# Block 3 of an output projection in a spare PSUM bank, and the last squares and the root of a norm moved behind the queries

## The chip, the cores and the metric

The kernel runs on one core of a Trainium2 chip. Five engines work side by side, each in the order of its own program: TensorE (PE, matrix products, with PEld for its weight loads), VectorE (DVE), ScalarE (ACT), GpSimd (POOL) and SyncE (SP, which issues transfers). They wait for each other through semaphores. The metric is the device time of one execution in microseconds, the median of the runs. PE sums products in PSUM, which has banks of 128 partitions by 512 float32 numbers.

## The reference

A trunk of two layers over x (512 positions by 1024 features) and a memory of 256 rows. All is float32:

```python
for layer in range(DEPTH):
    j = layer // 2
    xn = rms_norm(x, mix_norm[layer])
    if layer % 2 == 0:
        ...
        mixed = fox_diff_mixer(xn, attn_w_in[j], ..., attn_w_out[j], lambda_init)
    else:
        mixed = mlstm_mixer(xn, mlstm_w_in[j], ..., mlstm_w_out[j])
    x = x + mixed
    x = x + memory_cross_attention(rms_norm(x, xattn_norm[layer]), rms_norm(mem, mem_norm[layer]),
                                   xattn_wq[layer], xattn_wkv[layer], xattn_wo[layer])
    x = x + conv_ffn(rms_norm(x, ffn_norm[layer]), ...)
return rms_norm(x, final_norm)
```

Both mixers end in a product with an output matrix of 1024 by 1024 (called wo below), which is added to x. Then comes the memory attention, with four heads of 256 features:

```python
def memory_cross_attention(xn, memn, wq, wkv, wo):
    q = split_heads(xn @ wq, XATTN_HEADS)
    k, v = jnp.split(memn @ wkv, 2, axis=-1)
    ...
    logits = jnp.einsum('bhqd,bhmd->bhqm', q, k, preferred_element_type=jnp.float32) * (XATTN_HEAD_DIM ** -0.5)
    p = jax.nn.softmax(logits, axis=-1)
    out = jnp.einsum('bhqm,bhmd->bhqd', p.astype(v.dtype), v)
    return merge_heads(out) @ wo
```

The root in `rms_norm` is one number for each position. A query's root only scales its row of logits, so it isn't needed before the softmax.

## The kernel before

**Products.** A float32 product is made of three products of split operands: each operand is a high part (a cast, on ACT, L285) and a low part (the rest, on DVE, L282), and `mm3` issues high by high (L291), high weight by low operand (L292) and low weight by high operand (L293). x lies transposed in eight tiles x[0] to x[7] of 128 features by 512 positions.

**wo.** `p_out` makes wo in eight blocks m, one for each x[m]. A block is 24 products of 128x512 into one PSUM bank: three for each of the mixer's eight outputs. In layer 0 these outputs are the tiles mh and ml (the forgetting heads and the first differential ones), ka and, last, qa, which is cast from the last weighing (L1031, attention weights times values) straight before it is used. `xadd` (L619) adds the bank to x[m] and frees it. In layer 0, x[m] is first loaded again (`reload`). `xprep` then makes the high and low part of x[m] times the next gain, xh and xl (L603, L604), and `squares` (L589) adds the square of x[m] to a running sum sq: ACT squares (L597), DVE adds (L598).

**Banks.** There are four "acc" banks, which `p_proj` takes for its blocks. Two of them are held, from the mixer on, by "fills": keys of the memory attention that were made ahead (FILLS = 2), with two blocks m in each bank. So wo's blocks take turns on the other two. There are also two "s" banks and two "w" banks. In the mixer the w banks take transposes and weighings, later the first products X of each query.

**Queries.** `p_query` makes a head's query by a scheme with seven instead of eight products of quarters. `p1` and a second half make X in a w bank, `seed` (L1214, ACT) puts −X into an acc bank Y, and `p5`, `p6`, `p7`, `p3` and `p4` add products with sums of weights' quarters and sums of x's quarters. The sums of weights come from transfers that add (`sum_load`: sa, by SP and POOL), from `rest_load` (ra, SP) and from DVE (L1228, in `p6`); `kept` (L1224) copies what is needed twice to a tile xe. Heads 0 and 1 are "early": their first products run while wo isn't done. The sums of x's quarters ("forms", `p_forms`) are made for pairs of x tiles by ACT (L1489, L1498) and DVE (L1495 to L1497); the form of pair k lies in tile kv[k] (high) and kv[4 + k] (low, L282 kv). The last form needs x[7], which is block 8 of wo.

**Norm.** When sq is complete, `rsqrt_cols` sums it over the features by four float32 products with a matrix of ones (L452, to a bank s), and `rsqrt` makes the root y by twelve small DVE steps (L461 to L467). The scores first need y at L1418. A fill's keys are multiplied by the memory's root into a tile "tmp" (L1372) and split.

**Order.** The order of all this is set by a planner (`Plan`). Each piece of work is an item with what it needs, a priority (the lower number first), the banks and buffers that it takes and frees, and an estimate of its time on PE, ACT and DVE (`chain`). The planner writes the items out one after another; every engine then runs its part of that order. In the item of the norm, priority 2.5 puts it near the start of the queries.

## Time and profile before

| | us |
|---|---|
| runs: lowest, median, highest | 1457.26, 1458.25, 1460.52 |
| profiled execution | 1458.17 |
| its span, first to last instruction | 1456.4 |
| busy: PE | 1441.7 |
| busy: DVE | 1225.6 |
| busy: ACT | 986.1 |
| layer 0: wo's blocks 3 to 8 | from 228.48 to 261.26 |
| layer 0: root's sums on PE (L452) | at 268.81 |
| layer 0: first memory values (L352) | at 302.55 |
| layer 1: root's sums on PE (L452) | at 971.98 |

A row of the timeline gives the start of an instruction in us from the start of the span, its duration, the engine, the line, the operation, the tiles (out <- in) and a count; in brackets stands how long the engine had been idle and what ended that. The duration of a product is longer than its distance to the next one, since products overlap: distances tell what a product costs. The same holds for DVE, whose instructions of 0.68 us follow each other every 0.60.

### The profile page before, as it was taken

The page shows a single profiled execution, that of the slowest core. Times are in us where ns is not written, and L with a number is a line of the kernel's source. Part 1 is how long each engine was busy: PE and PEld are TensorE (multiplying, and loading weights), DVE is VectorE, ACT ScalarE, POOL GpSimd, SP SyncE. Part 2 cuts the span into 40 slices and gives each one's busy share as a digit, 9 for nine tenths or more (in the row PEclk, how much of TensorE's full clock was granted, in tenths as well). Part 3 has the DMA queues.
Part 4 walks back from the last instruction along what each step waited for, and adds up shares of the span by engine and source line. Part 5 has one row for each costly group of instructions (what it writes and reads, how often), then busy time and mean ns, then how long its engine had stood idle before and what let it go on. Part 6 is the DMA issues. An engine that isn't in the chain of part 4 may idle for free.

```text
span 1456.4 us, 24072 instructions
## 1 busy us (share of the span) xinstructions
PE 1441.7 (99%) x9019; PEld 1279.8 (88%) x9019; DVE 1225.6 (84%) x2223; ACT 986.1 (68%) x1776; POOL 73.3 (5%) x116
## 2 busy tenths in 40 slices
PE   9999999999999999999999999999999999999998
PEld 7888787998899999999888888889988999999987
DVE  7789987867899988889669988887779998888974
ACT  7689666655677777777547665566566777777764
POOL 0001120000000000000000100000000000000000
PEclk9999999999999999999999999999999999999999
DMA  5222336752246666562233332656414666666422
GB/s 200 87 74 73 117 119 199 171 177 88 94 128 163 183 158 161 150 163 74 84 101 109 109 110 65 204 142 189 131 48 119 160 179 172 156 160 156 105 67 79
DMA packets 70628, 190.24 MB, mean 131 GB/s; under 512 B 7520, under 2 KB 7520, under 8 KB 70512
## 3 DMA queue, kind: packets, MB, share of 16 engines
q1 hardware_dynamic: 62736, 162.17, 35.1%
q0 software_dynamic: 7200, 26.22, 10.7%
q8 instruction: 70, 1.15, 0.3%
q14 instruction: 46, 0.38, 0.1%
q10 hardware_dynamic: 576, 0.33, 0.1%
HBM read 186.56 MB, written 2.13 MB: 130 GB/s over the span
## 4 chain that ended last, share of the span: by engine, by line
PE 82%; DVE 10%; ACT 4%; issue 2%; DMA 1%; POOL 0%; DVEq 0%; SPq 0%; POOLq 0%; ACTq 0%
PE acc L291 15%; PE acc L292 15%; PE acc L293 14%; PE w L293 6%; PE w L291 6%; PE w L292 6%; PE s L293 3%; PE s L291 3%; PE s L292 3%; PE acc L352 2%; PE acc L354 2%; PE acc L353 2%; DVE wl L282 2%; DMA sa<-in_xq_dram 1%; DVE x L771 1%
## 5 line engine op out<-in xcount | busy, mean ns | idle before, releaser
L282 DVE TENSOR_TENSOR wl<-raw,wh 128x1024 fp32r<-128x1024 f32 (+3 forms) x181 | 213.9, 1182 | 41.2 <-ACT wh L285 32.3
L291 PE MATMUL acc<-xh,wh 128*128 128x256 f32 (+1 forms) x624 | 206.8, 331 | 0.1
L293 PE MATMUL acc<-xh,wl 128*128 128x256 f32 (+1 forms) x624 | 205.7, 330 | 0.1
L292 PE MATMUL acc<-xl,wh 128*128 128x256 f32 (+1 forms) x624 | 205.5, 329 | 0.0
L285 ACT CAST wh<-raw 128x1024 fp32r<-128x1024 f32 (+1 forms) x123 | 126.6, 1034 | 84.6 <-PE acc L292 43.0
L1676 DVE SCALAR_TENSOR_TENSOR c<-hs,vec,c 128x512 f32<-128x512 f32 x176 | 130.5, 749 | 15.9 <-ACT c L1669 14.0
L291 PEld LDWEIGHTS acc<-xh,wh 128*128 128x128 f32 x624 | 117.2, 188 | 12.1 <-ACT v L1917 0.6
L293 PEld LDWEIGHTS acc<-xh,wl 128*128 128x128 f32 x624 | 117.1, 188 | 12.0 <-DVE wl L282 0.5
L292 PEld LDWEIGHTS acc<-xl,wh 128*128 128x128 f32 x624 | 117.2, 188 | 11.5
L293 PE MATMUL w<-ah,wl 128*128 128x512 f32 x304 | 119.1, 392 | 0.0
L292 PE MATMUL w<-al,wh 128*128 128x512 f32 x304 | 118.6, 390 | 0.0
L291 PE MATMUL w<-ah,wh 128*128 128x512 f32 x304 | 118.5, 390 | 0.0
L282 DVE TENSOR_TENSOR wl<-sa,wh 128x1024 fp32r<-128x1024 f32 x52 | 63.6, 1222 | 17.0 <-ACT wh L1747 15.6
L1669 ACT ACTIVATE c<-hs,vec 128x512 f32<-128x512 f32 x88 | 71.2, 816 | 9.6 <-DVE hs L1816 8.2
L1747 ACT CAST wh<-sa 128x1024 fp32r<-128x1024 f32 x42 | 44.0, 1049 | 35.4 <-PE w L292 30.4
L293 PEld LDWEIGHTS w<-ah,wl 128*128 128x128 f32 x304 | 57.1, 188 | 12.0
L291 PEld LDWEIGHTS w<-ah,wh 128*128 128x128 f32 x304 | 57.1, 188 | 10.0 <-ACT w L1584 0.2
L292 PEld LDWEIGHTS w<-al,wh 128*128 128x128 f32 x304 | 57.0, 188 | 9.8
L282 DVE TENSOR_TENSOR s<-sb,s 128x512 fp32r<-128x512 f32 x92 | 63.1, 686 | 2.2 <-ACT s L285 0.3
L1554 ACT CAST wh<-dr 128x512 fp32r<-128x512 f32 x64 | 39.7, 621 | 34.1 <-PE w L292 32.2
L1732 POOL DMA_DIRECT2D sa<-in_up_dram x42 | 35.9, 855 | 515.7 <-DMA sa<-in_up_dram 173.9
L291 PE MATMUL acc<-mem,wh 128*128 128x256 f32 (+1 forms) x192 | 61.5, 320 | 0.0
(534 smaller groups left out, 4667.8 us busy)
## 6 DMA issues: line engine op xcount, KB each, us to landing
raw<-in_up_dram SPq DMA_DIRECT2D x46, 512.0 KB, 3.5
sa<-in_up_dram SPq DMA_DIRECT2D x42, 512.0 KB, 4.3
sa<-in_up_dram POOLq DMA_DIRECT2D x42, 512.0 KB, 5.7
dr<-in_down_dram SPq DMA_DIRECT2D x64, 256.0 KB, 2.7
ra<-in_up_dram SPq DMA_DIRECT2D x42, 256.0 KB, 3.0
raw<-in_xk_dram SPq DMA_DIRECT2D x16, 512.0 KB, 3.6
raw<-in_wo_dram SPq DMA_DIRECT2D x16, 512.0 KB, 3.5
raw<-in_xv_dram SPq DMA_DIRECT2D x16, 512.0 KB, 3.4
```

The lines of the kernel that those rows point to most:

```text
L282: self.nc.vector.tensor_tensor(out=lo, in0=v, in1=hi.bitcast(F32), op=ALU.subtract)
L285: self.nc.scalar.copy(hi, v)
L291: mm(out, wh, xh, start=first, stop=False, skip_group_check=parts)
L292: mm(out, wh, xl, start=False, stop=False, skip_group_check=parts)
L293: mm(out, wl, xh, start=False, stop=last, skip_group_check=parts)
L352: mm(ps, xh[k][:, ts], wh[:, ws], start=(k == 0), stop=False)
L353: mm(ps, xh[k][:, ts], wl[:, ws], start=False, stop=False)
L1554: nc.scalar.copy(st["wh"][:, :cols], st[tag][:, :cols])
L1669: nc.scalar.activation(st["c_"][:, j, :], hs()[:, j, 2:514], AF.Identity, scale=self.col("cw", (layer * 3 + 2) * 44 + blk), bias=self.col( ...
L1676: nc.vector.scalar_tensor_tensor(out=c, in0=hs()[:, j, n : n + 512], scalar=w, in1=c, op0=ALU.mult, op1=ALU.add)
L1732: return add("POOL", 0.0029 * cols, lambda: nc.gpsimd.dma_start(out(), src(), accum_op=ALU.add), deps, due, (), (), 6.0)
L1747: nc.scalar.copy(s["wh"][:, :cols], raw())
```

## The change

It has four parts.

1. In layer 0's wo, block m = 2 (block 3) takes a "w" bank in place of an acc bank, and its first products may be written ahead of the last products of blocks 1 and 2; they are put behind the items that make the mixer's output 3.
2. In the memory attention of both layers the squares of x[6] and x[7] leave `xprep`. They are made in a new function `inverse`, straight ahead of the root, in the tile "qs". That item's priority goes from 2.5 to 36.6, which is behind head 3's query.
3. For head 2, `p6` makes its sum in place in the first half of the raw tile ("pg") instead of in a tile "sb".
4. The fills' keys (m below 4) use a tile "xe" instead of "tmp".

```diff
@@ -302,7 +302,7 @@
             self.mm3(ps[:, :n], wh[:, s], wl[:, s], xh[k][:, :n], xl[k][:, :n], k == 0, k == nk - 1)
         return ps
 
-    def p_proj(self, pl, src, xs, evac, chain, deps=(), kdeps=None, edeps=(), prio=None, n=SEQ, nk=KB8, order=None, etake=(), per=2, eorder=(), load=(), off=0):
+    def p_proj(self, pl, src, xs, evac, chain, deps=(), kdeps=None, edeps=(), prio=None, n=SEQ, nk=KB8, order=None, etake=(), per=2, eorder=(), load=(), off=0, room="acc", behind=()):
 
         order = order or list(range(nk))
         st = {}
@@ -314,7 +314,7 @@
             def fn(c=c, ks=ks):
                 if c == 0:
                     st["w"] = self.weight(src, nk * P, off)
-                    st["ps"] = self.acc_bank(st["banks"][0])
+                    st["ps"] = self.acc_bank(st["banks"][0]) if room == "acc" else self.bank(room)
                 (wh, wl), (xh, xl) = st["w"], xs()
                 for j, k in enumerate(ks):
                     s = slice(k * P, (k + 1) * P)
@@ -325,10 +325,10 @@
                 d += (kdeps or {}).get(k, [])
             first = c == 0
             last = pl.add(
-                fn, 3 * len(ks) * MM * n / 512, d, prio, take=("acc", "wt") if first else (), free=("wt",) if e == nk else (),
-                pre=(("A", 0.12 * nk), ("D", 0.14 * nk)) if first else (), st=st,
+                fn, 3 * len(ks) * MM * n / 512, d, prio, take=(room, "wt") if first else (), free=("wt",) if e == nk else (),
+                pre=(("A", 0.12 * nk), ("D", 0.14 * nk)) if first else (), st=st, order=behind,
             )
-        return pl.add(lambda: evac(st["ps"]), 0, [last, *edeps], prio, take=etake, free=("acc",), chain=chain, order=eorder, load=load, st=st)
+        return pl.add(lambda: evac(st["ps"]), 0, [last, *edeps], prio, take=etake, free=(room,), chain=chain, order=eorder, load=load, st=st)
 
     def p_proj_tok(self, pl, src, xs, ntok, evac, deps=(), kdeps=None, edeps=(), prio=None, n=512, etake=(), ready=None, chain=None):
 
@@ -429,7 +429,8 @@
         done = []
         for m in range(KB8):
             e = self.p_proj(
-                pl, src[m], mixed, lambda ps, m=m: self.xadd(m, ps, reload), (("D", 0.6),), kdeps=kdeps, order=order, prio=prio + m
+                pl, src[m], mixed, lambda ps, m=m: self.xadd(m, ps, reload), (("D", 0.6),), kdeps=kdeps, order=order, prio=prio + m,
+                room="w" if reload and m == 2 else "acc", behind=kdeps[3] if reload and m == 2 else (),
             )
             done.append(
                 pl.add(lambda m=m: self.xprep(m, gain, gi, state), 0, [e], prio + m, chain=(("A", 0.52), ("D", 0.66), ("A", 0.52)), order=[order0])
@@ -586,14 +587,14 @@
         for t in range(4):
             self.nc.tensor.matmul(ps[:, 2 * t : 2 * t + 2], st["sq"][:, t * P : (t + 1) * P], self.ones2[:], start=True, stop=True)
 
-    def squares(self, k, v, n, state):
+    def squares(self, k, v, n, state, tmp=None):
 
         nc = self.nc
         if k == 0:
             state["sq"] = self.til(self.sp, "sq", bufs=1)
             nc.scalar.activation(state["sq"][:, :n], v, AF.Square)
         else:
-            tmp = self.til(self.sp, "sqt", bufs=2)
+            tmp = tmp or self.til(self.sp, "sqt", bufs=2)
             nc.scalar.activation(tmp[:, :n], v, AF.Square)
             nc.vector.tensor_tensor(out=state["sq"][:, :n], in0=state["sq"][:, :n], in1=tmp[:, :n], op=ALU.add)
 
@@ -611,7 +612,8 @@
             self.xh[k] = self.til(self.xp, f"xh{k}", dtype=F32R, bufs=1)
             self.xl[k] = self.til(self.xp, f"xl{k}", dtype=F32R, bufs=1)
             self.gained(k, self.x[k][:], self.col(gain, gi * 8 + k), self.xh[k][:], self.xl[k][:])
-        self.squares(k, self.x[k][:], SEQ, state)
+        if gain != "xat" or k < 6:
+            self.squares(k, self.x[k][:], SEQ, state)
 
     def xadd(self, m, ps, reload=False):
         if reload:
@@ -1224,7 +1226,7 @@
             nc.scalar.copy(st[n][:], st[bank][:, :256])
 
         def p6():
-            st["sb"] = self.til(mp, "qs", bufs=1) if h % 2 else self.til(self.kp, "sb", bufs=2)
+            st["sb"] = st["raw"][:, :512] if h == 2 else self.til(mp, "qs", bufs=1) if h % 2 else self.til(self.kp, "sb", bufs=2)
             tt_(out=st["sb"][:], in0=self.sums[h][:, 512:], in1=st["raw"][:, :512], op=ALU.add)
             if h == 0:
                 self.sum_load(layer, 2)
@@ -1312,9 +1314,13 @@
             self.formed.insert(0, pl.add(
                 last, 0, self.xdone[7], 0, order=self.formed[:], take=("hs", "hs"), free=("hs", "hs")
             ))
-            norm = pl.add(
-                lambda state=self.state: rs.append(self.rsqrt_cols(state["sq"], SEQ, 256.0 / DM, 256.0 * EPS)), 0.4, self.xdone[7], 2.5, take=("s",), free=("s",), chain=(("D", 2.3),)
-            )
+
+            def inverse(state=self.state):
+                for k in (6, 7):
+                    self.squares(k, self.x[k][:], SEQ, state, self.til(mp, "qs", bufs=1))
+                rs.append(self.rsqrt_cols(state["sq"], SEQ, 256.0 / DM, 256.0 * EPS))
+
+            norm = pl.add(inverse, 0.4, self.xdone[7], 36.6, take=("s",), free=("s",), chain=(("A", 1.04), ("D", 2.9)))
             mh, ml = [None] * 8, [None] * 8
             kd = {}
             kth, ktl, vh, vl, rs = [], [], [], [], []
@@ -1368,7 +1374,7 @@
                 for m in (2 * h, 2 * h + 1):
 
                     def keys(ps, m=m, at=0):
-                        tmp = self.til(mp, "tmp", (P, MEM))
+                        tmp = self.til(mp, "xe", (P, MEM), bufs=4) if m < 2 * len(self.fills) else self.til(mp, "tmp", (P, MEM))
                         nc.vector.tensor_tensor(out=tmp[:], in0=ps[:, at : at + MEM], in1=self.memrb, op=ALU.mult)
                         self.split(kth[m // 4][:, m % 4, :], ktl[m // 4][:, m % 4, :], tmp[:])
```

(The lines of the kernel after are two to six higher behind the edits: L1031 is L1033 there, L452 is L453, L604 is L605, L619 is L621, L1228 is L1230, and L1495 to L1497 are L1501 to L1503.)

**Layer 0, the end of the mixer, PE.** w_2628 is the bank of the last weighing; acc_481 and acc_510 are wo's blocks 1 and 2, qa_523 and qa_524 the high and low part of qa. Before:

```order
L1031 MATMUL w_2628<-pt_2554,v_1734 64x128
L291 MATMUL acc_481_2421<-qa_523_2637,wh_2416 128x512
L291 MATMUL acc_510_2547<-qa_523_2637,wh_2542 128x512
L292 MATMUL acc_481_2421<-qa_524_2638,wh_2416 128x512
L293 MATMUL acc_481_2421<-qa_523_2637,wl_2417 128x512
L292 MATMUL acc_510_2547<-qa_524_2638,wh_2542 128x512
L293 MATMUL acc_510_2547<-qa_523_2637,wl_2543 128x512
L291 MATMUL acc_549_2689<-mh_128,wh_2684 128x512
```

After, with block 3 in w_2647:

```order
L1033 MATMUL w_2628<-pt_2554,v_1734 64x128
L291 MATMUL w_2647<-mh_128,wh_2642 128x512
L292 MATMUL w_2647<-ml_134,wh_2642 128x512
L293 MATMUL w_2647<-mh_128,wl_2643 128x512
L291 MATMUL w_2647<-mh_129,wh_2642 128x512
L292 MATMUL w_2647<-ml_135,wh_2642 128x512
L293 MATMUL w_2647<-mh_129,wl_2643 128x512
L291 MATMUL acc_481_2421<-qa_523_2637,wh_2416 128x512
L292 MATMUL acc_481_2421<-qa_524_2638,wh_2416 128x512
L293 MATMUL acc_481_2421<-qa_523_2637,wl_2417 128x512
L291 MATMUL acc_510_2547<-qa_523_2637,wh_2542 128x512
```

Six products of block 3 have moved ahead of the six products with qa; the other 18 follow behind these.

**Layer 0, from the last add of x to the last form, DVE.** x_145 is x[7], hs_3036 (before) and hs_3044 (after) are the last form's sums, and kv_534 and kv_538 its low half. Before:

```order
L619 TENSOR_TENSOR x_145<-acc_591_2919,x_145 128x512
L1228 TENSOR_TENSOR qs_3148<-sa_2798,raw_2979 128x512
L282 TENSOR_TENSOR wl_3045<-sa_2665,wh_3044 128x1024
L604 SCALAR_TENSOR_TENSOR xl_600_2973<-x_145,vec,xh_599_2972 128x512
L598 TENSOR_TENSOR sq_2681<-sq_2681,sqt_2976 128x512
L1495 TENSOR_TENSOR hs_3036<-hs_3035 128x512
L1228 TENSOR_TENSOR sb_3301<-sa_3060,pg_3261 128x512
L1496 TENSOR_TENSOR hs_3036<-hs_3035,hs_3036 128x256
L1372 TENSOR_TENSOR tmp_3507<-acc_434_2161,memrb_1758 128x256
L1497 TENSOR_TENSOR hs_3036<-hs_3035,hs_3036 128x256
L1372 TENSOR_TENSOR tmp_3511<-acc_434_2161,memrb_1758 128x256
L282 TENSOR_TENSOR kv_534_2659<-hs_3036,kv_530_2655 128x1024
```

After:

```order
L621 TENSOR_TENSOR x_145<-acc_589_2910,x_145 128x512
L1230 TENSOR_TENSOR qs_3121<-sa_2772,raw_2969 128x512
L282 TENSOR_TENSOR wl_3030<-sa_2678,wh_3029 128x1024
L605 SCALAR_TENSOR_TENSOR xl_604_3000<-x_145,vec,xh_603_2999 128x512
L1501 TENSOR_TENSOR hs_3044<-hs_3043 128x512
L1502 TENSOR_TENSOR hs_3044<-hs_3043,hs_3044 128x256
L1503 TENSOR_TENSOR hs_3044<-hs_3043,hs_3044 128x256
L282 TENSOR_TENSOR kv_538_2672<-hs_3044,kv_534_2668 128x1024
```

The square's add, head 2's sum and the fill's two keys have left this stretch; they stand further back.

**Layer 0, the root's sums, PE.** acc_598 is the acc bank of an early head's query, acc_665 that of head 3's; w_2957 is an X, and acc_696 holds memory values. Before:

```order
L291 MATMUL acc_598_2970<-kv_529_2654,s_626_3063 128x256
L292 MATMUL acc_598_2970<-kv_533_2658,s_626_3063 128x256
L293 MATMUL acc_598_2970<-kv_529_2654,s_626_3063 128x256
L452 MATMUL s_3075<-ones_82,sq_2681 128x2 x4
L291 MATMUL w_2957<-xh_599_2972,wh_2953 128x256
```

After:

```order
L292 MATMUL acc_665_3371<-kv_538_2672,a_675_3455 128x256
L293 MATMUL acc_665_3371<-kv_534_2668,a_675_3455 128x256
L453 MATMUL s_3477<-ones_82,sq_2700 128x2 x4
L352 MATMUL acc_696_3520<-wh_3515,mem_1514 128x512
L353 MATMUL acc_696_3520<-wl_3516,mem_1514 128x512
```

The four products stood between products of the early heads; they now stand behind the last product of head 3's query and ahead of the memory values.

## Prediction

> **What bounds the kernel now.** I read the page's busy shares and clock first, then the waits of TensorE (PE), then the timeline of PE, ScalarE (ACT) and VectorE (DVE) at the two places that the change touches. On the page, and in the view of cores:
>
> ```profile
> PE 1441.7 (99%) x9019; PEld 1279.8 (88%) x9019; DVE 1225.6 (84%) x2223; ACT 986.1 (68%) x1776; POOL 73.3 (5%) x116
> core 0: 1456.4 us, clock 0.999
> ```
>
> PE is busy for 1441.7 of the span's 1456.4 us, at full granted clock throughout, so the change can win only what PE stands still, and can lose without such a limit. Its number of instructions is the same on every engine. One line of the waits view of PE (total, times, longest), and PE at the end of layer 0's mixer, with ACT and DVE beside it (columns: start, duration, engine, line, operation, count, and the idle time before it with what ended it):
>
> ```profile
> PE s L291 <- ACT xe L1224: 0.6, 2, 0.3
> 222.56 3.00 PE L1031 MATMUL w<-pt,v 128*64 128x512 f32 x16
> 226.24 0.73 PE L291 MATMUL acc<-qa,wh 128*128 128x512 f32 x2 [0.68 <-ACT qa L285]
> 228.48 0.50 PE L291 MATMUL acc<-mh,wh 128*128 128x512 f32 x1 [0.33 <-DVE x L619]
> 234.06 0.39 PE L291 MATMUL acc<-mh,wh 128*128 128x512 f32 x1
> 239.50 0.39 PE L291 MATMUL acc<-mh,wh 128*128 128x512 f32 x1
> 223.18 0.29 DVE L805 COPY pt<-w 128x128 f32<-128x128 f32 x1 [0.83 <-ACT pt L803]
> 225.60 0.58 ACT L285 CAST qa<-w 128x512 fp32r<-128x512 f32 x1 [2.46 <-PE w L1031]
> 226.22 0.69 DVE L282 TENSOR_TENSOR qa<-w,qa 128x512 fp32r<-128x512 f32 x1 [2.75 <-ACT qa L285]
> 227.50 2.00 ACT L285 CAST wh<-raw 128x1024 fp32r<-128x1024 f32 x2 [1.31 <-PE acc L292]
> 228.94 1.22 DVE L282 TENSOR_TENSOR wl<-raw,wh 128x1024 fp32r<-128x1024 f32 x1
> 236.72 0.69 DVE L1228 TENSOR_TENSOR sb<-sa,sa 128x512 f32<-128x512 f32 x1 [2.81 <-DMA sa<-in_xq_dram]
> 237.33 0.68 DVE L619 TENSOR_TENSOR x<-acc,x 128x512 f32<-128x512 f32 x1
> ```
>
> PE finishes the last weighing at 225.56, waits for its cast to the qa pair, runs the six products left of wo's blocks 1 and 2, and waits again until the add of x frees a bank for block 3 at 228.48. A block is 24 products in 239.50 − 234.06 = 5.44 us, 0.227 each.
>
> **Part 1: block 3 in a w bank.** By the order, six products of block 3, on the operands mh and ml that are long there, now stand between the last weighing and the qa products. The w bank that they take was last copied out at 223.18 + 0.29 = 223.47, so nothing holds them up. They start about 225.45 and take 6 × 0.227 = 1.36, to 226.81. The qa high part is ready at 225.60 + 0.58 = 226.18. The low part is ready at 226.22 + 0.69 = 226.91; its first product comes second, at 227.04. The six qa products end at 228.17 and the other 18 of block 3 run without a wait, since the bank is theirs already: end near 228.2 + 18 × 0.227 = 232.3, against 234.06. Gain 1.76 us; the two waits alone (0.68 + 0.33 = 1.01) are its lower end if the uneven spacing in between stays, 1.8 the upper one. I take 1.76, because the order leaves nothing between the products.
>
> *Next wait there.* The weights of blocks 4 and 5 are cast at 227.50, when blocks 1 and 2 let their buffers go; that becomes about 228.2, and block 4's low part, 1.44 + 1.22 behind it as before (227.50 to 228.94 and on), is ready near 230.9, ahead of 232.3. DVE is the nearer limit. By its windows it is full behind this place:
>
> ```profile
> 240.00:244.00 4.00, 4.00 (x19) 3.33 (x18) 4.00 (x6) 3.07 (x4) 0.00 (x0) 1.00 0.51 171
> ```
>
> (The window: length, then busy time and count of PE, weight loads, DVE, ACT, POOL; clock; DMA share; GB/s.) But just ahead of it DVE stood 2.81 us for sa at 236.72 while the add at 237.33 was already due. In the new order that sum stands five rows further back, behind that add and its weights' split, so DVE starts the full stretch with up to 2.8 us more done; 1.76 of this is needed.
>
> By the Trainium skill, "TensorE: Matmul & The Clock Gate", section "Wait — 56ns, not 53.3ns?", warm products of 512 columns start every 215.7 ns; the blocks here show 227. By its figure the six products would cover 1.29 and not 1.36, and the estimate of this part would be 0.07 smaller; the measured spacing stands.
>
> **Part 2: the last two squares and the root.** The places are these, in PE's, ACT's and DVE's timeline of layer 0:
>
> ```profile
> 261.03 0.39 PE L293 MATMUL acc<-qa,wl 128*128 128x512 f32 x1
> 262.67 0.28 PE L291 MATMUL w<-xh,wh 128*128 128x256 f32 x1
> 265.13 0.28 PE L293 MATMUL w<-xh,wl 128*128 128x256 f32 x1
> 265.53 0.39 PE L291 MATMUL w<-xh,wh 128*128 128x256 f32 x1
> 268.81 0.95 PE L452 MATMUL s<-ones,sq 128*128 128x2 f32 x8
> 269.62 0.36 PE L291 MATMUL w<-xh,wh 128*128 128x256 f32 x1
> 270.65 0.35 PE L292 MATMUL s<-kv,wh 128*128 128x256 f32 x1
> 272.06 0.39 PE L291 MATMUL s<-xh,s 128*128 128x256 f32 x1 [0.31 <-ACT xe L1224]
> 302.55 0.40 PE L352 MATMUL acc<-wh,mem 128*128 128x512 f32 x1
> 265.11 0.36 ACT L1214 ACTIVATE acc<-w 128x256 f32<-128x256 f32 x1
> 262.33 0.68 DVE L619 TENSOR_TENSOR x<-acc,x 128x512 f32<-128x512 f32 x1
> 265.33 0.68 DVE L598 TENSOR_TENSOR sq<-sq,sqt 128x512 f32<-128x512 f32 x1
> 265.93 0.69 DVE L1495 TENSOR_TENSOR hs<-hs 128x512 f32<-128x512 f32 x1
> 266.54 0.69 DVE L1228 TENSOR_TENSOR sb<-sa,pg 128x512 f32<-128x512 f32 x1
> 267.47 0.42 DVE L1372 TENSOR_TENSOR tmp<-acc,memrb 128x256 f32<-128x256 f32 x1
> 267.81 0.42 DVE L1497 TENSOR_TENSOR hs<-hs,hs 128x256 f32<-128x256 f32 x1
> 268.14 0.42 DVE L1372 TENSOR_TENSOR tmp<-acc,memrb 128x256 f32<-128x256 f32 x1
> 269.34 1.23 DVE L282 TENSOR_TENSOR kv<-hs,kv 128x1024 fp32r<-128x1024 f32 x1 [0.78 <-ACT kv L1498]
> 315.85 0.15 DVE L1418 TENSOR_TENSOR sm<-sm,y 128x1 f32<-128x1 f32 x1
> ```
>
> L452, the four products of the root's sums, costs PE 269.62 − 268.81 = 0.81 us at its old place, and I price it the same behind head 3's p4 (302.55 in this trace): net 0. It runs back to back in both orders, so its end there is nothing else's start. (The same page and section give about 25 ns as the floor between starts: by that, eight passes would be 0.2 us and the new place could return 0.6 per layer; 0.81 over eight is 101 ns, so the row denies it.)
>
> What matters is that L452 stood ahead of a wait that is just not seen. The low half of the last form, kv lo, ends at 269.34 + 1.23 = 270.57, and its first product starts at 270.65. If PE comes 1.76 earlier by part 1 and 0.81 earlier without L452, kv lo must come as much earlier or PE stands for it. Its chain from the add at 262.33 is 8.24 us, DVE without a pause. The new order takes out of it one square's add (265.33 to 265.93, 0.60), the sum sb (of the same size, 0.60) and two keys' products (267.47 to 267.81, 0.34 each): 1.88 of DVE's time, of which I count 1.6, since the cast of kv's high half lies in between: 8.24 − 1.6 = 6.65. The add itself waits for block 8's last product. By the order 12 products of 256 columns now stand ahead of block 8's last three; 12 such are the stretch from 261.26 (0.227 after block 8's last start at 261.03) to 262.67, where the second weights' products begin: 1.41. The add therefore comes at about 262.33 − 1.76 + 1.41 − 0.9 = 261.1, where 0.9 is what it stood in DVE's queue (block 8's last product ran out at 261.03 + 0.39 = 261.4). So kv lo is ready at 261.1 + 6.65 = 267.8; PE arrives at 270.65 − 1.76 − 0.81 − 0.28 = 267.8, where 0.28 is the wait for the seed in front of 265.53 (0.40 after 265.13 against 0.12), which goes since the seed is due earlier against PE's row. The margin is nil, but no loss. The xe wait at 272.06 I keep.
>
> Sum of layer 0: 1.76 + 0.28 = 2.04, with L452's 0.81 taken out at 269 and paid at 300.
>
> *The root late.* Its y is first needed at 315.85. In the new order the two squares' adds and the twelve small steps follow head 3's p4 on DVE: L452 ends near 301.2, and with the splits between them y is there near 305; the first scores come 2.04 earlier than now, at 313.8. Some 8 us cover it. ACT gets the two squares (0.6 each) around the seed of head 3; if that seed waited for one of them, PE would lose up to 0.6 per layer. I take 0, and put it into the upper end.
>
> **Parts 3 and 4: head 2's sum in its raw tile, the fills' keys in xe tiles.** No instruction more; the sum and keys lose the wait for a shared buffer and move back. The in-place sum costs DVE its 0.68 as before. SP now issues the third rest load ahead of pg's; the transfer is 256 KB, pg is read only by head 2's casts, several us behind its landing. Cost nothing, between 0 and the 0.6 of one cast.
>
> **Layer 1.** Wo is as before there; only parts 2 to 4 apply:
>
> ```profile
> 968.55 0.28 PE L293 MATMUL w<-xh,wl 128*128 128x256 f32 x1
> 968.79 0.39 PE L291 MATMUL w<-xh,wh 128*128 128x256 f32 x1
> 971.98 0.95 PE L452 MATMUL s<-ones,sq 128*128 128x2 f32 x8
> 973.81 0.28 PE L292 MATMUL s<-kv,wh 128*128 128x256 f32 x1
> 971.99 1.23 DVE L282 TENSOR_TENSOR kv<-hs,kv 128x1024 fp32r<-128x1024 f32 x1 [0.79 <-ACT kv L1498]
> ```
>
> Kv lo ends at 973.22, with PE due at 973.81 − 0.81 = 973.0; shortened by 1.6 it ends at 971.6 and is no wait. The 0.12 lost ahead of 968.79 (0.24 after 968.55 against 0.12) goes, and I give as much again to the shorter chain: gain 0.25, bounds 0 and, with the xe wait's 0.3, 0.55.
>
> **Sum.** 2.04 + 0.25 = 2.3 off the profiled execution's 1458.17 (0.08 below the runs' median of 1458.25): 1455.9 us for the median, 0.16% less. 0.2%, 2.9 us, is about what a measurement of this kernel can tell from no change, so this counts as "same".
>
> **Rivals.**
>
> *A: the xe waits go too.* They are 0.6 in both layers; with the uneven starts around them in part 1's ratio (1.76 against 1.01) 1.05: 1458.25 − 2.3 − 1.05 = 1454.9, faster by 0.2%. For it: ACT and DVE lose work ahead of xe's copies. Against: PE comes there earlier too.
>
> *B: part 1's gain is lost at kv lo.* If the add at 262.33 comes only 0.5 earlier, because DVE is full from 240 on, kv lo is ready at 268.4 and PE loses 0.6: 1456.5; with the chain unshortened as well, 1.7: 1457.6.
>
> *C: slower: L452 was the cover.* If block 8's last three products, now 1.41 later in the row, hold the add at 262.33 or behind it and the chain keeps its 8.24, kv lo stays at 270.57: PE wins nothing before it, and each layer's 0.81 is paid uncovered at 300 and 1004: 1458.25 + 1.6 = 1459.9; with the seed of head 3 late by 0.6 twice, 1461. It decides once kv lo comes less than 0.81 earlier than 270.57. Against it: the order takes 1.87 of DVE work out of the chain. For it: the full windows.
>
> **How the numbers follow.** Forecast 0.48 (1455.0 to 1456.9), A 0.22, B 0.15, C 0.15. Faster by over 0.2% (below 1455.33) is most of A and the forecast's lower edge: 0.27. Slower by over 0.2% (above 1461.17) is the far half of C, and what the order cannot show: 0.13. The rest is 0.60. The range goes from A with the runs' scatter (0.5), 1454.3, to C's first number less its last tenths, 1459.4.
>
> **What would show it.** Right: no wait between the weighings and the qa products, block 4 starting near 232.3, values near 300.5, kv lo's wait below 0.2, L452 behind p4 with the same 0.81. Wrong: PE idle for DVE kv L282 ahead of the forms' last products, or for ACT's seed L1216 in head 3; a wait of block 4 to 8 for x or wl; the first scores waiting for y.

## The result and the profile after

The changed kernel takes 1455.97 us (median of 10 runs, 1455.32 to 1456.33) against 1458.67 us for the kernel before (10 runs, 1457.26 to 1461.39): a ratio of 0.998, 95% interval 0.997 to 0.9989. That is 0.19% faster: clear of noise by this interval, and just short of the 0.2% that the prediction set as its bound. The two profiled executions differ by less than the medians do, 1456.33 against 1458.17, 1.84 us: the execution profiled before was half a microsecond under its median, the one profiled after, the slowest of its ten, 0.36 above its own. The kernel before also scatters more; what the runs show of that stands below.

The page's first lines, two lines of the waits view of PE (total, times, longest), and the timeline of PE in the kernel after:

```profile
span 1454.5 us, 24074 instructions
PE 1440.7 (99%) x9019; PEld 1280.2 (88%) x9019; DVE 1226.8 (84%) x2223; ACT 986.6 (68%) x1776; POOL 74.7 (5%) x116
...
PE s L291 <- ACT xe L1226: 0.3, 1, 0.3
PE s L292 <- DVE kv L282: 0.2, 1, 0.2
...
222.37 3.01 PE L1033 MATMUL w<-pt,v 128*64 128x512 f32 x16
225.31 0.50 PE L291 MATMUL w<-mh,wh 128*128 128x512 f32 x1
226.81 0.39 PE L291 MATMUL acc<-qa,wh 128*128 128x512 f32 x1
232.28 0.39 PE L291 MATMUL acc<-mh,wh 128*128 128x512 f32 x1
...
267.60 0.28 PE L291 MATMUL acc<-kv,s 128*128 128x256 f32 x1
268.12 0.39 PE L292 MATMUL s<-kv,wh 128*128 128x256 f32 x1 [0.24 <-DVE kv L282]
...
269.13 0.39 PE L291 MATMUL s<-xh,s 128*128 128x256 f32 x1
...
299.87 0.95 PE L453 MATMUL s<-ones,sq 128*128 128x2 f32 x8
300.68 0.48 PE L352 MATMUL acc<-wh,mem 128*128 128x512 f32 x1
...
1003.79 0.49 PE L352 MATMUL acc<-wh,mem 128*128 128x512 f32 x1
```

The last of these in the kernel before:

```profile
1005.71 0.40 PE L352 MATMUL acc<-wh,mem 128*128 128x512 f32 x1
```

The waits for the qa cast (0.7) and for the add of x ahead of block 3 (0.3) are gone. Products of block 3 start right behind the weighing, and block 4 starts at 232.28. A short new wait for kv lo stands at 268.12; this was one of the prediction's signs of being wrong, and it came at 0.24 us.

The same landmarks in both profiles; what stands ahead of the edit differs by 0.19 already at the last weighing (its start lies between 222.12 and 223.14 in the thirteen profiles here), so the last column counts from there:

| PE | before | after | difference | less 0.19 |
|---|---|---|---|---|
| last weighing (L1031 / L1033) | 222.56 | 222.37 | −0.19 | 0 |
| block 4 of wo | 234.06 | 232.28 | −1.78 | −1.59 |
| first product that needs kv lo | 270.65 | 268.12 | −2.53 | −2.34 |
| behind the wait for xe | 272.06 | 269.13 | −2.93 | −2.74 |
| first memory values, layer 0 | 302.55 | 300.68 | −1.87 | −1.68 |
| first memory values, layer 1 | 1005.71 | 1003.79 | −1.92 | −1.73 |
| span | 1456.4 | 1454.5 | −1.9 | −1.7 |

Nearly all that is won is won in layer 0 between 222 and 303. The row behind xe stands 2.74 earlier; 0.81 of this is L452, which is paid back ahead of the values. Another 0.25 is lost on the way there, and no wait in that stretch shows where. DVE in the same stretch of the kernel after:

```profile
237.14 0.69 DVE L1230 TENSOR_TENSOR sb<-sa,sa 128x512 f32<-128x512 f32 x1
261.11 0.69 DVE L621 TENSOR_TENSOR x<-acc,x 128x512 f32<-128x512 f32 x1 [1.79 <-PE acc L293]
266.84 1.23 DVE L282 TENSOR_TENSOR kv<-hs,kv 128x1024 fp32r<-128x1024 f32 x1 [1.11 <-ACT kv L1504]
304.32 0.17 DVE L468 SCALAR_TENSOR_TENSOR y<-a,y 128x4 f32<-128x4 f32 x1
313.96 0.15 DVE L1424 TENSOR_TENSOR sm<-sm,y 128x1 f32<-128x1 f32 x1
```

x[7]'s add is no longer late in DVE's queue: DVE stood idle for 1.79 us and waited for block 8. Kv lo ends at 266.84 + 1.23 = 268.07. The root y is ready at 304.49, 9.5 us ahead of its first use at 313.96.

### The profile page after: what moved, and what is told of

Read it like the earlier page. It is cut to its first block, busy times and chain, and to the rows that moved or that the text cites. A ratio compares the mean times of both kernels' runs of the same rounds, so it can differ in the third digit from the quotient of the medians.

```text
span 1454.5 us, 24074 instructions
## 1 busy us (share of the span) xinstructions
PE 1440.7 (99%) x9019; PEld 1280.2 (88%) x9019; DVE 1226.8 (84%) x2223; ACT 986.6 (68%) x1776; POOL 74.7 (5%) x116
## 4 chain that ended last, share of the span: by engine, by line
PE 85%; DVE 9%; ACT 4%; issue 2%; DMA 1%; POOL 0%; DVEq 0%; SPq 0%; ACTq 0%; POOLq 0%
PE acc L291 15%; PE acc L292 15%; PE acc L293 15%; PE w L293 6%; PE w L292 6%; PE w L291 6%; PE s L293 3%; PE s L291 3%; PE s L292 3%; PE acc L352 2%; PE acc L354 2%; PE acc L353 2%; DVE wl L282 2%; DVE x L773 1%; DVE c L1682 1%
## 5 line engine op out<-in xcount | busy, mean ns | idle before, releaser
L282 DVE TENSOR_TENSOR wl<-raw,wh 128x1024 fp32r<-128x1024 f32 (+3 forms) x181 | 214.2, 1184 | 36.6 <-ACT wh L285 27.6
```

The lines of the kernel that those rows point to most:

```text
L282: self.nc.vector.tensor_tensor(out=lo, in0=v, in1=hi.bitcast(F32), op=ALU.subtract)
```

## The experiments

All were timed beside the kernel before. "sd" is the standard deviation of the kernel's own runs; that of before was 0.82 to 0.88 in the three groups of runs (27 to 35 runs each), that of the whole change 0.33 (10 runs, in the earlier group of the result, where before had 1.21 in 10 runs). Before's median went from 1458.67 in that group to 1458.26 in the last, so "above the whole change" below compares two groups and is uncertain by some 0.4.

| kernel | median, us (range, runs) | ratio to before | 95% interval | sd |
|---|---|---|---|---|
| part 1 alone | 1457.43 (1456.66 to 1458.72, 11) | 0.9992 | 0.9983 to 1.0 | 0.66 |
| part 2 alone | 1459.85 (1457.78 to 1463.81, 12) | 1.0011 | 1.0002 to 1.0021 | 2.10 |
| parts 3 and 4 alone | 1460.38 (1458.99 to 1462.39, 11) | 1.0012 | 1.0004 to 1.0021 | 0.87 |
| all but part 1 | 1457.15 (1456.64 to 1458.34, 11) | 0.999 | 0.9981 to 0.9998 | 0.51 |
| all but part 2 | 1457.96 (1456.92 to 1458.81, 11) | 0.9995 | 0.9986 to 1.0004 | 0.56 |
| all but part 3 | 1457.75 (1456.93 to 1463.35, 11) | 1.0001 | 0.9992 to 1.001 | 1.75 |
| all but part 4 | 1456.65 (1455.96 to 1457.61, 11) | 0.9989 | 0.998 to 0.9998 | 0.54 |
| whole change, root early | 1458.31 (1457.49 to 1459.33, 11) | 0.9998 | 0.9989 to 1.0007 | 0.49 |
| before, root alone late | 1458.50 (1457.51 to 1461.58, 11) | 1.0006 | 0.9997 to 1.0014 | 1.33 |
| before, sa later | 1457.79 (1457.29 to 1458.58, 11) | 0.9997 | 0.9988 to 1.0006 | 0.37 |
| whole change, sa later | 1456.92 (1455.87 to 1458.66, 11) | 0.9992 | 0.9983 to 1.0001 | 0.82 |

Differences of under a microsecond between two medians are near what these runs can tell, so the verdicts below rest on the profiles, place by place. What a profile gains or loses in layer 0 is counted from the start of the last weighing to the first memory values (79.99 before), in layer 1 from the first product behind wo to the first memory values (40.93 before). Kernels with the same edits in layer 1 differ there by up to 0.5, so less than that says little.

### Part 1 alone

Against the kernel before, only this (and the parameters `room` and `behind`):

```diff
-                pl, src[m], mixed, lambda ps, m=m: self.xadd(m, ps, reload), (("D", 0.6),), kdeps=kdeps, order=order, prio=prio + m
+                pl, src[m], mixed, lambda ps, m=m: self.xadd(m, ps, reload), (("D", 0.6),), kdeps=kdeps, order=order, prio=prio + m,
+                room="w" if reload and m == 2 else "acc", behind=kdeps[3] if reload and m == 2 else (),
```

> Part 1 alone (block 3 in a w bank; squares, root, head 2's sum and the fills' keys as before). Theory (the gain at wo is kept only if kv lo, the low half of the last form, comes as much earlier): block 3 ends 1.6 us earlier against the last weighing, but in DVE's order the chain from x[7]'s add to kv lo keeps the square's add, the sum and the two keys and even gets six of the root's small steps, so kv lo is ready near 270.0 while PE would be there at 269.05: PE waits about 1.0, and 0.6 of 1.6 us is left; time about 0.6 us below before. Rival (part 1 is worth its own gain wherever the rest stands): 1.6 to 1.8 us below before, no wait for DVE kv.

1457.43, 1.2 under the 1458.62 of before; in the profile it gains 0.99 in layer 0. The gain at wo is there (1.58 at block 4); a good third of it is lost ahead of the forms' last products, as the theory has it, but most of the waiting there is not for kv lo:

```profile
268.09 0.16 DVE L462 TENSOR_SCALAR z<-s 128x4 f32<-128x4 f32 x1 [0.81 <-PE s L453]
...
269.98 0.38 PE L291 MATMUL s<-kv,wh 128*128 128x256 f32 x1 [0.90 <-ACT wh L285]
270.50 0.38 PE L292 MATMUL s<-kv,wh 128*128 128x256 f32 x1
```

PE waits 0.90 for a cast of weights (ACT was held behind the chain's own cast) and stands again, 0.52 between two rows that are 0.12 apart elsewhere, until kv lo. DVE itself waits in the chain for L453's sums. A stall that is removed upstream comes back where the next late producer is.

### Part 2 alone

Squares and root as in the whole change, wo, head 2's sum and the keys as before:

```diff
+        if gain != "xat" or k < 6:
+            self.squares(k, self.x[k][:], SEQ, state)
...
+            norm = pl.add(inverse, 0.4, self.xdone[7], 36.6, take=("s",), free=("s",), chain=(("A", 1.04), ("D", 2.9)))
```

> Part 2 alone (last two squares and the root behind head 3's query). Theory: L452's 0.81 us leave a place where they were cover and come back behind p4; kv lo is 0.6 us earlier (one square's add less), PE 0.81 earlier, so it waits 0.1 to 0.2 in layer 0 and not in layer 1: time within 0.3 us of before. Rival (the root's sums are worth their 0.81 in each layer): 1.6 us below before.

Neither theory: 1459.85, slower, and with the widest scatter of all. DVE's chain and PE behind it:

```profile
267.17 0.69 DVE L1229 TENSOR_TENSOR sb<-sa,pg 128x512 f32<-128x512 f32 x1 [1.04 <-DMA pg<-in_xq_dram]
...
270.00 0.38 PE L291 MATMUL s<-kv,wh 128*128 128x256 f32 x1 [0.56 <-ACT kv L1503]
271.26 0.39 PE L292 MATMUL s<-kv,wh 128*128 128x256 f32 x1 [0.88 <-DVE kv L282]
...
970.83 0.69 DVE L1229 TENSOR_TENSOR sb<-sa,pg 128x512 f32<-128x512 f32 x1 [1.30 <-DMA pg<-in_xq_dram]
...
974.92 0.39 PE L292 MATMUL s<-kv,wh 128*128 128x256 f32 x1 [0.87 <-DVE kv L282]
```

In the order of this kernel SP issues the third rest load ahead of pg's, as in the whole change. Head 2's sum still stands in the middle of the chain to kv lo, and now waits 1.04 us for pg to land; everything behind it on DVE waits too. PE, which comes 0.81 earlier without L452, waits 0.56 and 0.88, and pays L452 later. Layer 1, where the theory expected no wait, shows the same.

### Parts 3 and 4 alone

```diff
-            st["sb"] = self.til(mp, "qs", bufs=1) if h % 2 else self.til(self.kp, "sb", bufs=2)
+            st["sb"] = st["raw"][:, :512] if h == 2 else self.til(mp, "qs", bufs=1) if h % 2 else self.til(self.kp, "sb", bufs=2)
...
-                        tmp = self.til(mp, "tmp", (P, MEM))
+                        tmp = self.til(mp, "xe", (P, MEM), bufs=4) if m < 2 * len(self.fills) else self.til(mp, "tmp", (P, MEM))
```

> Parts 3 and 4 alone (head 2's sum in place, the fills' keys in xe tiles). Theory: kv lo comes about 1.3 us earlier, but PE does not wait for it as long as L452 stands ahead: time within 0.2 us of before. Rival (DVE's load in this stretch is what costs): 0.5 us or more below before.

Neither theory again: 1460.38, 1.8 above before. The profile has two causes:

```profile
237.11 0.69 DVE L1228 TENSOR_TENSOR sb<-sa,sa 128x512 f32<-128x512 f32 x1 [3.40 <-DMA sa<-in_xq_dram]
...
262.73 0.68 DVE L619 TENSOR_TENSOR x<-acc,x 128x512 f32<-128x512 f32 x1
...
264.49 0.39 PE L291 MATMUL w<-xh,wh 128*128 128x256 f32 x1 [0.45 <-ACT acc L1214]
...
283.19 0.36 PE L291 MATMUL acc<-kv,a 128*128 128x256 f32 x1 [0.37 <-DVE hs L1197]
...
987.46 0.36 PE L291 MATMUL acc<-kv,a 128*128 128x256 f32 x1 [0.37 <-DVE hs L1197]
```

One is the change's own: by the new order eight products of a later X stand earlier on PE, and at 283 and 987 PE waits for a difference (hs, L1197) that DVE makes behind other work. In the profile layer 1 loses 0.9 us in this stretch, of which such waits are the visible part. The other is no part of the change: DVE waited 3.40 us for sa where it waited 2.81 in the profile of before, though SP issued the load at the same place (0.48 behind the last weighing's start), and x[7]'s add came as much later. It belongs to this one execution and so does not explain the median. It is followed up below.

### All but part 1

The whole change without the two lines of part 1:

```diff
-                room="w" if reload and m == 2 else "acc", behind=kdeps[3] if reload and m == 2 else (),
```

> Everything but part 1. Theory: only the small waits ahead of kv lo go (0.1 to 0.3 in each layer), L452's 0.81 is paid later: 0.2 to 0.5 us below before, with the waits for the qa cast and for the add of x still there (0.68 and 0.33). Rival (part 2 carries the gain): 1.5 us or more below before.

1457.15, 1.5 under the 1458.62 of before: not the 0.2 to 0.5 of the theory, but the rival's number. The profile gains 0.74 in layer 0 and 0.43 in layer 1. So parts 2 to 4, which lose by themselves (part 2, and parts 3 and 4), win together. By the order, part 3 takes head 2's sum out of the chain, so pg may land late, and with part 2 the eight products of a later X are not put forward, so the wait for hs does not arise. The whole change is 1.2 us better by the medians and 0.94 by layer 0's profile (1.68 less 0.74): that is what part 1's 1.59 is worth with the rest.

### All but one of parts 2, 3 and 4

The whole change with the old root and squares:

```diff
-            norm = pl.add(inverse, 0.4, self.xdone[7], 36.6, take=("s",), free=("s",), chain=(("A", 1.04), ("D", 2.9)))
+            norm = pl.add(lambda state=self.state: rs.append(self.rsqrt_cols(state["sq"], SEQ, 256.0 / DM, 256.0 * EPS)), 0.4, self.xdone[7], 2.5, take=("s",), free=("s",), chain=(("D", 2.3),))
...
-        if gain != "xat" or k < 6:
-            self.squares(k, self.x[k][:], SEQ, state)
+        self.squares(k, self.x[k][:], SEQ, state)
```

> Everything but part 2 (parts 1, 3 and 4): the root's sums stay ahead of the last form's products, the squares stay in xprep. If the root's move is worth nothing by itself, as the prediction's sum has it (L452's 0.81 leaves and comes back), the time is within 0.4 us of the whole change, 1456.0. Theory after the first four runs: parts 3 and 4 without part 2 cost 0.8 to 0.9 us in each layer near head 2's query (a wait of PE for DVE hs L1197 and for ACT's seed), so the gain of part 1 (1.6 less about 0.4 at kv lo) is eaten: time within 0.7 us of before, with these two waits in both layers.

1457.96, 2.0 above the whole change: the theory of the first four runs holds for layer 1 (1.01 lost there against before's profile, with the same wait of 0.37 for DVE hs at 985.16), while layer 0 does not show that wait and keeps 1.1. So the root's move is worth more than the nothing that the prediction's sum gave it.

Without part 3:

```diff
-            st["sb"] = st["raw"][:, :512] if h == 2 else self.til(mp, "qs", bufs=1) if h % 2 else self.til(self.kp, "sb", bufs=2)
+            st["sb"] = self.til(mp, "qs", bufs=1) if h % 2 else self.til(self.kp, "sb", bufs=2)
```

> Everything but part 3: head 2's sum in a tile of its own, which puts it back into the chain from x[7]'s add to kv lo. SP issues pg's load behind the third rest load, so the sum also waits for pg's landing, as in part 2 alone (1.04 us). Theory: kv lo 0.6 to 1.6 us later in each layer, and PE, which had no margin there, waits as much longer: 1.2 to 3 us above the whole change. Rival (part 3 is worth nothing): within 0.3 us of it.

1457.75 by the median, 1.8 above the whole change, with single runs up to 1463.35. In layer 1 the sum waits for pg and PE for kv lo; layer 0 of the same profile stands above it:

```profile
239.12 0.69 DVE L1230 TENSOR_TENSOR sb<-sa,sa 128x512 f32<-128x512 f32 x1 [1.54 <-DMA sa<-in_xq_dram]
...
261.47 0.69 DVE L621 TENSOR_TENSOR x<-acc,x 128x512 f32<-128x512 f32 x1 [0.71 <-PE acc L293]
...
970.68 0.69 DVE L1230 TENSOR_TENSOR sb<-sa,pg 128x512 f32<-128x512 f32 x1 [1.51 <-DMA pg<-in_xq_dram]
...
974.56 0.38 PE L292 MATMUL s<-kv,wh 128*128 128x256 f32 x1 [0.87 <-DVE kv L282]
```

In layer 0 the sum waited only 0.23 for pg. The sum for head 0 waited 1.54 for sa there, and x[7]'s add is not later for it (38.71 behind the last weighing's start, 38.74 in the whole change): DVE still stood idle ahead of it. Both kernels in which head 2's sum stands ahead of kv lo behind a late pg scatter most (sd 2.10 and 1.75).

Without part 4:

```diff
-                        tmp = self.til(mp, "xe", (P, MEM), bufs=4) if m < 2 * len(self.fills) else self.til(mp, "tmp", (P, MEM))
+                        tmp = self.til(mp, "tmp", (P, MEM))
```

> Everything but part 4: the fills' keys in the tile tmp. By the order two DVE steps (one of them 0.34 us in the middle of the chain) come back ahead of kv lo. Theory: kv lo 0.3 to 0.7 later and PE's wait for it as much longer in layer 0, less in layer 1 (0.9 margin): 0.3 to 0.9 us above the whole change. Rival: within 0.2 us of it.

1456.65, 0.68 above the whole change, in the theory's range. But the profiles do not bear out the size: this one's span is 1454.4 against 1454.5, and layer 0 loses 0.37 against the whole change. Nor does PE wait for kv lo there; it waits 0.87 for a cast of weights behind the chain's:

```profile
268.47 0.38 PE L291 MATMUL s<-kv,wh 128*128 128x256 f32 x1 [0.87 <-ACT wh L285]
```

### The root back at its place

```diff
-            norm = pl.add(inverse, 0.4, self.xdone[7], 36.6, take=("s",), free=("s",), chain=(("A", 1.04), ("D", 2.9)))
+            norm = pl.add(inverse, 0.4, self.xdone[7], 2.5, take=("s",), free=("s",), chain=(("A", 1.04), ("D", 2.9)))
```

> The whole change with the root's priority back at 2.5: the last two squares are still made straight ahead of the root, but root and squares stand early. L452's 0.81 is again PE's work ahead of kv lo, and the squares' adds are in the chain. Theory: PE arrives 0.81 later, kv lo 0.6 to 1.2 later; the wait for kv lo stays near 0.4, so the time is within 0.5 us of the whole change: not the root's place, but the length of the chain decides. Rival (the late root is what wins): 0.8 us or more above the whole change in each layer, 1457.6 or higher.

1458.31: the theory falls, and the rival holds: against the whole change the profile loses 1.08 us in layer 0 and 1.06 in layer 1. In layer 0 PE waits for a cast of weights, in layer 1 for hs, as in the two kernels with parts 3 and 4 and an early root:

```profile
270.64 0.39 PE L291 MATMUL w<-xh,wh 128*128 128x256 f32 x1 [0.71 <-ACT wh L285]
...
985.53 0.35 PE L291 MATMUL acc<-kv,a 128*128 128x256 f32 x1 [0.35 <-DVE hs L1199]
```

What the late root brings is thus not L452's own 0.81, which is paid in either place, but the order that the planner writes with it.

### The root alone late

The kernel before with priority 36.6 for its root, squares where they were:

```diff
-                lambda state=self.state: rs.append(self.rsqrt_cols(state["sq"], SEQ, 256.0 / DM, 256.0 * EPS)), 0.4, self.xdone[7], 2.5, take=("s",), free=("s",), chain=(("D", 2.3),)
+                lambda state=self.state: rs.append(self.rsqrt_cols(state["sq"], SEQ, 256.0 / DM, 256.0 * EPS)), 0.4, self.xdone[7], 36.6, take=("s",), free=("s",), chain=(("D", 2.3),)
```

> The kernel before with the root alone moved behind head 3's query: squares, head 2's sum, keys and wo as before, and pg's load still ahead of the third rest load. Theory (L452 was cover for the wait on kv lo, rival C of the prediction): in layer 0 PE comes 0.81 earlier to a kv lo that stays where it was, waits about 0.7 for it, and pays L452 later: 0.75 us lost; in layer 1 0.2 to 0.4 lost; 0.9 to 1.2 us above before. Other theory (L452 only changes its place): within 0.2 us of before.

1458.50, 0.24 above before and inside the interval of no difference; the loss of 0.9 to 1.2 is not there. But the spread is (sd 1.33 against 0.82), and the profiled run, at 1457.52 among the fastest of its eleven, shows why it can't decide:

```profile
234.23 0.69 DVE L1228 TENSOR_TENSOR sb<-sa,sa 128x512 f32<-128x512 f32 x1 [0.66 <-DMA sa<-in_xq_dram]
...
261.12 0.69 DVE L619 TENSOR_TENSOR x<-acc,x 128x512 f32<-128x512 f32 x1
```

In this execution sa landed early, DVE waited 0.66 us and not 2.81, and x[7]'s add came at 38.90 us behind the last weighing's start (222.22) where it came at 39.77 before. Kv lo was early enough for the 0.81, and PE did not wait for it. That PE waits when sa lands late would fit the wide spread, but no slow execution of this kernel was profiled, so it is not shown.

### What sa's landing does

In the kernel before, the order puts DVE's sum sb for head 0 ahead of x[2]'s add, so DVE waits for sa there. The kernels with that order and the same work behind it, counted from the start of the last weighing:

| kernel | sum sb starts at | x[7]'s add starts at |
|---|---|---|
| before, root alone late | 12.01 | 38.90 |
| before | 14.16 | 39.77 |
| parts 3 and 4 alone | 14.75 | 40.37 |

Between the last two, a landing 0.59 later makes the add 0.60 later, 25 us on: DVE has no pause in between. Between the first two, 2.15 of landing make 0.87 of add, because with the early landing DVE does pause, for PE. Two runs tested it. In both, layer 0's load of sa is issued behind the first quarter's and the first rest load:

```diff
-            self.sum_load(layer, 0)
+            if layer:
+                self.sum_load(layer, 0)
+            sa = None if layer else self.til(self.kp, "sa", (P, 1024), bufs=3)
             self.first = self.til(self.kp, "sa", (P, 1024), bufs=3)
             self.nc.sync.dma_start(self.first[:], self.t["xq"][layer, 0])
             self.rest_load(layer, 0)
+            if not layer:
+                self.sum_load(layer, 0, sa)
```

In the kernel before this also moves the sum seven rows back on DVE, behind x[2]'s add:

> The kernel before with layer 0's first weights' sum (sa) issued behind the first quarter's and the first rest load; by the order DVE's sum sb for head 0 then stands seven rows further back, behind x[2]'s add and what hangs on it, as the whole change has it. Theory (before, DVE stood 2.8 to 3.5 us for sa's landing and was full from there to x[7]'s add, so that landing set the add's time): no wait of DVE for sa ahead of x[2]'s add, x[7]'s add 0.5 to 0.9 us earlier, the wait for head 1's seed (0.28) gone: 0.3 to 0.8 us below before, and the runs closer together than those of before (standard deviation 0.85). Other theory (sa's landing is hidden): within 0.2 us of before, same spread.

The median is 0.47 lower (1457.79), as the theory has it but within the interval of no difference, and the scatter falls from 0.82 to 0.37. DVE's wait for sa stands at another place and x[7]'s add comes at 262.04 − 223.14 (the last weighing's start there) = 38.90:

```profile
240.65 0.69 DVE L1232 TENSOR_TENSOR sb<-sa,sa 128x512 f32<-128x512 f32 x1 [1.23 <-DMA sa<-in_xq_dram]
...
262.04 0.69 DVE L619 TENSOR_TENSOR x<-acc,x 128x512 f32<-128x512 f32 x1
```

In the whole change, where the sum stands back already, the later issue only makes the landing later:

> The whole change with the same later issue of sa; no other engine's order differs. Theory: DVE waits 1 to 3 us at the sum, but it stood idle for 1.79 us ahead of x[7]'s add, so at most a part of it comes through: within 0.5 us of the whole change, 1456.0. Other theory (the delay goes through as in the kernel before): 1 us or more above it.

```profile
240.19 0.69 DVE L1234 TENSOR_TENSOR sb<-sa,sa 128x512 f32<-128x512 f32 x1 [2.89 <-DMA sa<-in_xq_dram]
...
260.68 0.38 PE L292 MATMUL w<-xl,wh 128*128 128x256 f32 x1 [0.47 <-DVE xl L605]
...
261.92 0.69 DVE L621 TENSOR_TENSOR x<-acc,x 128x512 f32<-128x512 f32 x1
```

Of 2.89 us of wait, x[7]'s add is 0.74 later (39.48 behind the last weighing's start against 38.74 in the whole change); the idle time ahead of it is used up, and PE waits 0.47 for a low part of x that DVE makes late. The time rises by 0.95 (by 1.36 if each is set against before in its own group), more than expected and near the other theory, and sd to 0.82. So the slack of DVE is some 2 us (2.89 less 0.74, beside 1.79 of idle time), and beyond it the landing decides again.

## Why the prediction was right, and where its steps were not

The forecast was 1455.9, the measured median 1455.97, inside the range; the chance of 0.60 for "same" was given to the case that came. The agreement to a tenth is partly chance: the sum said 2.3 off the profiled execution, and the profiled executions differ by 1.84; the medians differ by 2.70, because the kernel before had been profiled in an execution 0.50 faster than its median and the kernel after in one 0.36 slower. The forecast's base, the median of three runs (1458.25), was 0.42 under the later median of ten, and its gain 0.4 under that of the medians; the two errors cancel.

- **Part 1.** 1.76 forecast, 1.59 measured at block 4. The start of the qa products, forecast at 226.81, is 226.81 in a profile that runs 0.19 ahead. The term that was mis-sized is the six products of block 3: they take 1.50 (225.31 to 226.81), not 1.36.
- **DVE's lead.** It held: forecast, x[7]'s add at 261.1; measured 261.11 (261.30 with the 0.19), with 1.79 us of idle time ahead of it.
- **Kv lo.** Forecast ready at 267.8 with PE there at the same time, "the margin is nil, but no loss". It ends at 268.07, and PE stands 0.52 at a place where rows are 0.12 apart: 0.4 lost. This term was mis-sized too: from x[7]'s add to kv lo's end the chain takes 6.96 (261.11 to 268.07), 0.31 more than the 6.65 counted. The order took 1.28 out of the 8.24, not 1.6: with a key's product gone, DVE waits 1.11 and not 0.78 for the cast of kv's high half.
- **The seed.** 0.28 forecast to go; in the kernel after PE still stands about 0.2 there. In return the wait for xe, which the forecast kept, shrank: 0.31 between 268.82 and 269.13 where 0.59 stood before. That is half of rival A: of 0.6 us of waits for xe, layer 0's 0.3 went and layer 1's stayed. Layer 0: 2.04 forecast, 1.68 measured.
- **L452.** 300.68 − 299.87 = 0.81 at the new place, the price assumed; the eight passes cost nothing less behind p4.
- **The root late.** y at 304.5, needed at 314.0: covered, as worked out.
- **Layer 1.** 0.25 forecast. From the first products behind wo (964.78 before) to the first values the profile gains about 0.2; the kernel without part 1 and the whole change with sa later, whose edits in layer 1 are the same, gain 0.43 and lose 0.06 there. The forecast lies within this spread, which is too wide to confirm it.
- **Parts 3 and 4.** "Cost nothing" held for the whole change, but its reason was read wrongly. Pg is not read "only by head 2's casts": head 2's sum reads it too, and it doesn't wait only because part 3 has moved it back (to 272.71). Without part 3 the sum waits 0.23 to 1.51 us for pg and the time is 1.8 above the whole change. And alone parts 3 and 4 stand 1.8 above before. The prediction added up the parts one by one; it did not see that these two make part 2 pay, and part 2 them.
- **Rival C** named a mechanism that shows only where kv lo is itself late: in part 2 alone, where its chain waits for pg, PE waits 0.56 and 0.88 there. Moving the root alone lost only 0.24, not shown to differ from zero, and its profile has no wait for kv lo; that this depends on when sa lands is likely but not shown.
- **Rival B's** loss of part 1's gain at kv lo is what part 1 does alone, where 0.99 of 1.58 is kept, though most of the wait is for a cast of weights.

What the prediction did not see at all is that in the kernel before x[7]'s add hung on a transfer. It read DVE's 2.81 us of waiting as room, not as something that differs from one execution to another.

## What to carry to other kernels

A stall taken out upstream is worth only what the next late producer is moved too: follow the chain from the edit to the next wait, and count the work on each engine in it. Parts of a change can each lose and win together, so an edit is judged with the order that it makes, its DMA issues among it, and not by its own instructions. Where an engine without a pause waits for a transfer, that landing sets everything behind it; moving the waiting instruction back until there is work ahead of it brought the runs closer together here; that it also made them faster is not shown (0.47 us, within the interval).

## What was not expected of the hardware

The landing of one transfer differs from execution to execution by more than the change is worth: with the same order on SP and DVE up to it, the sum that waits for sa started 12.01, 14.16, 14.75, 14.85 and 14.89 us behind the last weighing's start in the profiles of five kernels, one execution each. In the kernel without part 3, where SP issues the load at the same place, it was 16.36.

The spread of the run times follows in part. In six kernels where DVE had other work ahead of the sum that needs sa, and the chain to kv lo did not wait for pg, the standard deviations are 0.33 to 0.66; with sa issued later in the whole change, which that work does not cover, it is 0.82. In three where the sum comes first they are 0.82 to 0.88 (before), 0.87 (parts 3 and 4) and 1.33 (the root alone late). Where the chain that PE waits for held a sum that waits for pg, they are 1.75 and 2.10. But the kernel without part 1 also has the sum first (3.50 us of wait in its profile) and scatters by 0.51 only. The two runs that moved the load (0.82 to 0.37, and 0.33 to 0.82) point to the landing of sa as a cause of the scatter, but that it is the cause in each kernel is not shown.
